# Dropping the allowance for late operands from the planner that orders a decoder block's instructions

## The chip, the cores and the metric

The kernel runs on one NeuronCore of a Trainium2 chip. The metric is the device time of one execution in microseconds (us), median of the runs shown. One profiled execution gives the trace that all rows below come from. PE is TensorE's matmul, PEld its weight load, DVE is VectorE, ACT is ScalarE, POOL is GpSimd, SP is SyncE, whose queue (SPq) issues the transfers. [...]

## The reference

One hybrid decoder layer over 1024 tokens of width 1024, in float32:

```python
xn = rms_norm(x, norm1_g)
q, k, v, p_rw = split(xn @ w_in)
attn = rms_norm(dilated_attention(q, k, v, ...))     # 8 heads of 64, three dilations
rwkv = rwkv7_time_mix(p_rw, ...)                     # 8 heads of 64, a scan over the tokens
x = x + concat(attn, rwkv) @ w_out
xn2 = rms_norm(x, norm2_g)
out = x + (silu(xn2 @ w_gate) * (xn2 @ w_up)) @ w_down
```

The scan keeps a 64x64 state for each head and updates it token by token. The kernel does it in chunks of 64 tokens, so that a chunk is a few matrix products, but one chunk still needs the state that the chunk before it left.

## The kernel before

**Stages.** First come the norm of x and the in-projection (`inproj`, line 524), 26 column blocks by two halves of the tokens; each product of 512 columns is split into three passes of a rounded high and low part. Beside it runs the scan. It has 8 units (four pairs of heads by two halves of the tokens), each prepared by `decays`, `keys`, `scoring`, `sides`, `turn`, `invert` and `merge` (lines 674 to 935) and then walked through by `chain` (line 937), 8 chunks in each unit. Then come attention (`attend`, `near`, `far`, lines 1140 to 1313), the output projection (`outproj`, line 1442) in two rounds, the second norm, and the feed-forward part (`ffproj`, line 1659, then `down`, line 1762), which is the second half of the span.

**The chain.** In each chunk the state goes through three round trips between TensorE and another engine. The product with the state (`chain<-S,ra` in the trace) is copied to Rb by DVE; the product of Rb (`chain<-Rb,M`) is copied to VS by DVE and to Ub by ACT; the products of VS and Ub (`chain<-VS,kbT`, `chain<-Ub,M`) give the new S by DVE, which the next chunk's first product reads. `post` (line 993) turns a unit's result into a part of the mix that the output projection reads.

**The order.** Nothing is scheduled by the compiler; the program itself writes each engine's instructions out in one order, and each engine then takes its own list in that order, with semaphores for the data. The order comes from `Flow`, a list planner that runs while the program is built. Every stage is a generator (a stream) with a rank, a low number being more urgent: norms 2, `feed` 2.5, `chain` 3, the other steps of the scan 3.1 to 3.6, `attn_load` 3.7 and `fetch_wo` 3.8, the workers of attention 8.2 and up, `inproj` 9, `outproj` 9.5. In a loop `Flow.run` (line 237) asks each stream when its next instruction could start (`Flow.ready`, line 180), takes the most urgent of those that could start at the planned time, and otherwise the one that could start first. `Flow.issue` (line 202) books the instruction's planned cost on its engine. So `inproj` fills whatever time TensorE has left.

**When an operand is ready.** For an operand that another engine wrote, `ready` adds to the writer's planned end a lag by engine (line 48) and, if the reader is TensorE, 60 ns and the allowance `LATE`:

```python
LAG = {"PE": 200, "ACT": 145, "DVE": 140, "POOL": 65, "SP": 1500}
LATE, SWITCH = 300, 100
...
r = max(r, t + LAG[e] + (60 + LATE if op.eng == "PE" else 0))
```

A TensorE instruction is thus put into the list where the planner holds its operand to be 300 ns old, beyond the lags. The result is both the place in the order and the planned start, so that what depends on it is planned later too.

**Memory and the joints.** `flow.run(dense)` (line 1346) plans until the in-projection is done. Only then are its pools closed, and the pools of attention are opened in the room that it had: four score buffers, two buffers of queries, three of values. `flow.run(rwkv)` (line 1361) plans on until the scan is done; then the scan's pools are closed, attention gets four more score buffers, and the loads of the output projection (`fetch_wo`, `mix_load`, `residual`) are added. Both kernels have these joints and pools.

Of the kernel before, what the change touches and what calls it, by code (L numbers as in the profile page):

```python
# [47 lines left out]
LAG = {"PE": 200, "ACT": 145, "DVE": 140, "POOL": 65, "SP": 1500}  # L48


LATE, SWITCH = 300, 100
OWN = {"PE": 0, "ACT": 100, "DVE": 130, "POOL": 95, "SP": 900}


# [49 lines left out]
class Flow:  # L104
# [75 lines left out]
    def ready(self, s):  # L180
        op = s.head
        if isinstance(op, Wait):
            if any(m not in self.marks for m in op.marks):
                return None
            return max((self.marks[m] for m in op.marks), default=0.0)
        if isinstance(op, Get):
            t, n = sorted(self.free[op.kind].values()), op.n or 1
            return t[n - 1] if len(t) >= n else None
        r = self.clk.get(op.eng, 0.0)
        if op.eng == "SP":  # L190
            r = max(r, self.clk.get("queues", 0.0) - 3000)
        for keys, which in ((op.rd, 0), (op.wr, 0), (op.wr, 1)):
            for k in keys:
                if k in self.slots:
                    for e, t in self.slots[k][which].items():
                        if e != op.eng or (e == "SP" and (keys is op.rd or which)):
                            r = max(r, t + LAG[e] + (60 + LATE if op.eng == "PE" else 0))
                        elif keys is op.rd and which == 0:
                            r = max(r, t + OWN[e])
        return r  # L200
# [1659 lines left out]
```

## Time and profile before

| What | Value |
|---|---|
| median of 3 runs | 1493.05 us (1490.79 to 1494.58) |
| profiled execution, its own time | 1501.24 us |
| its span, first to last instruction | 1499.4 us |
| PE busy | 1426.3 us, 95% of the span |
| PEld, DVE, ACT, POOL busy | 77%, 53%, 48%, 36% |
| mean granted clock | 0.973 |

A stretch is given as its start and end in us from the first instruction. "Busy" is the time in which an engine executes; the end of a matmul is modelled. A wait row names the engine that waited, the tile that it was to write, and who released it; only idle time of the waiting engine counts in it. Since every instruction is recorded by one helper (line 235, in `Flow.emit`), all rows carry this line, and tiles are what tells the stages apart.

### The profile page before, as it was taken

The page shows a single profiled execution, that of the slowest core. Times are in us where ns is not written, and L with a number is a line of the kernel's source. Part 1 is how long each engine was busy: PE and PEld are TensorE (multiplying, and loading weights), DVE is VectorE, ACT ScalarE, POOL GpSimd, SP SyncE. Part 2 cuts the span into 40 slices and gives each one's busy share as a digit, 9 for nine tenths or more (in the row PEclk, how much of TensorE's full clock was granted, in tenths as well). Part 3 has the DMA queues.
Part 4 walks back from the last instruction along what each step waited for, and adds up shares of the span by engine and source line. Part 5 has one row for each costly group of instructions (what it writes and reads, how often), then busy time and mean ns, then how long its engine had stood idle before and what let it go on. Part 6 is the DMA issues. An engine that isn't in the chain of part 4 may idle for free. (4 is left out here: it accounts for less than half of the span.)

```text
span 1499.4 us, 24765 instructions
## 1 busy us (share of the span) xinstructions
PE 1426.3 (95%) x8710; PEld 1155.9 (77%) x8710; DVE 801.1 (53%) x1799; ACT 714.3 (48%) x1768; POOL 539.8 (36%) x564
## 2 busy tenths in 40 slices
PE   8999989999999986799999899999999999999999
PEld 5677767777778865688888678888888888888887
DVE  5456677657656337666776734443444434334334
ACT  5434556576676775555855433333333333333332
POOL 4432344255645451422454733444444440000000
PEclk8999999999999988799999999999999999999999
DMA  5343222323323344998521222222222224445443
GB/s 192 108 120 75 65 82 78 99 76 110 115 87 103 105 150 125 276 248 224 151 63 50 84 78 85 85 83 79 75 79 80 85 77 134 148 148 197 148 148 126
DMA packets 199789, 173.83 MB, mean 116 GB/s; under 512 B 39025, under 2 KB 150897, under 8 KB 199666
## 3 DMA queue, kind: packets, MB, share of 16 engines
q1 hardware_dynamic: 199666, 172.26, 38.3%
q8 instruction: 69, 1.13, 0.3%
q14 instruction: 54, 0.44, 0.1%
HBM read 130.26 MB, written 37.75 MB: 112 GB/s over the span
## 5 line engine op out<-in xcount | busy, mean ns | idle before, releaser
L235 ACT ACTIVATE oph<-fraw 128x512 fp32r<-128x512 f32 x208 | 126.3, 627 | 228.7 <-PE chain L235 97.9
L235 POOL TENSOR_TENSOR opl<-fraw,oph 128x512 fp32r<-128x512 f32 x76 | 99.6, 1315 | 220.6 <-PE bank L235 71.3
L235 DVE TENSOR_TENSOR opl<-fraw,oph 128x512 fp32r<-128x512 f32 x132 | 87.5, 689 | 143.6 <-ACT oph L235 143.6
L235 ACT ACTIVATE oph<-sw 128x512 fp32r<-128x512 f32 x80 | 50.6, 632 | 179.4 <-DVE sw L235 71.5
L235 POOL TENSOR_TENSOR inlo<-inraw,inhi 128x512 fp32r<-128x512 f32 x62 | 82.2, 1326 | 84.8 <-ACT inhi L235 70.6
L235 PE MATMUL bank<-opl,oph 128*128 128x512 f32 x176 | 68.5, 389 | 0.0
L235 PE MATMUL bank<-oph 128*128 128x512 f32 x176 | 68.5, 389 | 0.0
L235 PE MATMUL bank<-oph,opl 128*128 128x512 f32 x176 | 68.5, 389 | 0.0
L235 DVE TENSOR_TENSOR opl<-sw,oph 128x512 fp32r<-128x512 f32 x80 | 56.0, 699 | 21.0 <-ACT oph L235 17.2
L235 DVE TENSOR_TENSOR uu<-bank,uu 128x512 f32<-128x512 f32 x20 | 13.8, 692 | 81.7 <-PE bank L235 81.7
L235 DVE SCALAR_TENSOR_TENSOR S<-chain,ec,Sp 64x64 f32<-64x64 f32 x112 | 31.6, 282 | 43.1 <-PE chain L235 38.5
L235 ACT ACTIVATE Ub<-chain 64x64 f32<-64x64 f32 x128 | 28.2, 220 | 54.6 <-DVE VS L235 52.4
L235 POOL TENSOR_TENSOR sw<-fraw 128x512 f32<-128x512 f32 x40 | 52.0, 1299 | 0.0
L235 ACT ACTIVATE Y<-chain 64x64 f32<-64x64 f32 x128 | 26.9, 212 | 51.1 <-DVE S L235 45.8
L235 ACT ACTIVATE inhi<-inraw 128x512 fp32r<-128x512 f32 x62 | 38.7, 624 | 16.7 <-DMA inraw<-in_w_in_dram 6.7
L235 DVE COPY Rb<-chain 64x64 f32<-64x64 f32 x128 | 28.9, 226 | 27.9 <-PE chain L235 25.4
L235 POOL TENSOR_TENSOR up<-up,sg 128x512 f32<-128x512 f32 x20 | 32.3, 1617 | 30.1 <-POOL sw L235 16.1
L235 ACT ACTIVATE sb<-sb,mx 128x256 f32<-128x256 f32 (+3 forms) x64 | 36.2, 567 | 14.4 <-DVE mx L235 14.3
L235 PEld LDWEIGHTS bank<-oph,opl 128*128 128x128 f32 x176 | 33.0, 188 | 6.9
L235 PEld LDWEIGHTS bank<-oph 128*128 128x128 f32 x176 | 33.0, 188 | 6.8
L235 PEld LDWEIGHTS bank<-opl,oph 128*128 128x128 f32 x176 | 33.0, 188 | 6.8
L235 POOL TENSOR_TENSOR rsf<-smf,nhalf 128x8 f32<-128x8 f32 x16 | 26.6, 1662 | 31.6 <-DVE smf L235 31.3
(494 smaller groups left out, 4228.6 us busy)
## 6 DMA issues: line engine op xcount, KB each, us to landing
fraw<-in_w_down_dram SPq DMA_DIRECT2D x88, 256.0 KB, 2.8
inraw<-in_w_in_dram SPq DMA_DIRECT2D x62, 256.0 KB, 2.9
fraw<-in_w_gate_dram SPq DMA_DIRECT2D x48, 256.0 KB, 3.7
fraw<-in_w_up_dram SPq DMA_DIRECT2D x48, 256.0 KB, 3.0
fraw<-h_d SPq DMA_DIRECT2D x44, 256.0 KB, 2.9
h_d<-up SPq DMA_DIRECT2D x42, 256.0 KB, 2.1
rkv_d<-stage SPq DMA_DIRECT2D x24, 256.0 KB, 2.9
xt<-in_x_dram SPq DMA_DIRECT2D x8, 512.0 KB, 7.3
```

The source lines that it names most:

```text
L235: op.fn(*op.a, **op.k)
```

## The change

`LATE` is dropped. A TensorE instruction's operand then counts as ready 60 ns plus the writer's lag after the writer's planned end, without the further 300 ns. Nothing else in the program is edited; the same instructions are issued with the same operands, in the order that the planner then writes.

```diff
-LATE, SWITCH = 300, 100
+SWITCH = 100
 OWN = {"PE": 0, "ACT": 100, "DVE": 130, "POOL": 95, "SP": 900}
...
                         if e != op.eng or (e == "SP" and (keys is op.rd or which)):
-                            r = max(r, t + LAG[e] + (60 + LATE if op.eng == "PE" else 0))
+                            r = max(r, t + LAG[e] + (60 if op.eng == "PE" else 0))
                         elif keys is op.rd and which == 0:
```

## Rows read from the trace of the kernel before

**Rows 1.** The page's head: span, and busy time of each engine.
```profile
span 1499.4 us, 24765 instructions
PE 1426.3 (95%) x8710; PEld 1155.9 (77%) x8710; DVE 801.1 (53%) x1799; ACT 714.3 (48%) x1768; POOL 539.8 (36%) x564
```

**Rows 2.** Busy time by stretch: length, engines, granted clock, DMA share, GB/s.
```profile
50.00:550.00 500.00, 479.68 (x4218) 379.05 (x4216) 300.85 (x742) 299.62 (x855) 230.91 (x234) 0.99 0.33 97
550.00:600.00 50.00, 32.11 (x179) 26.60 (x177) 31.43 (x103) 27.59 (x98) 10.10 (x10) 0.80 0.46 133
600.00:850.00 250.00, 227.66 (x1311) 192.74 (x1312) 179.77 (x512) 153.71 (x429) 112.75 (x154) 0.92 0.59 160
850.00:1500.00 650.00, 645.40 (x2821) 529.02 (x2819) 262.95 (x399) 205.26 (x338) 165.18 (x124) 1.00 0.34 108
```

**Rows 3.** The same view, 550 to 600 us in steps of 10 us.
```profile
550.00:560.00 10.00, 5.85 (x25) 4.42 (x24) 2.91 (x10) 7.14 (x23) 4.39 (x5) 0.63 0.44 141
560.00:570.00 10.00, 8.47 (x46) 7.58 (x46) 7.08 (x28) 5.28 (x21) 2.39 (x3) 0.69 0.78 232
570.00:580.00 10.00, 6.67 (x50) 5.41 (x48) 8.76 (x27) 7.54 (x25) 1.30 (x2) 1.00 0.70 188
580.00:590.00 10.00, 7.14 (x40) 6.03 (x39) 6.10 (x20) 5.00 (x18) 0.00 (x0) 0.84 0.36 104
590.00:600.00 10.00, 3.98 (x25) 3.17 (x24) 6.58 (x20) 2.62 (x14) 2.01 (x2) 0.84 0.00 1
```

**Rows 4.** Tiles of in-projection, attention and chain: durations, first and last start.
```profile
L235 PE MATMUL mm<-xn11l,inhi x104: 388/393/628, 53.7 to 547.1; 128*128 128x512 f32 x104
L235 PE MATMUL bank<-kk,qv x104: 222/336/735, 563.6 to 748.8; 128*128 128x128 f32 x44, 128*128 128x384 f32 x24, 128*128 128x256 f32 x20, 128*128 128x512 f32 x16
L235 DVE COPY Rb<-chain x128: 183/227/229, 129.9 to 590.8; 64x64 f32<-64x64 f32 x128
```

**Rows 5.** Instructions in order of time, one round trip at 301 us.
```profile
301.57 0.47 DVE L235 COPY Rb<-chain 64x64 f32<-64x64 f32 x2 [0.52 <-PE chain L235]
...
302.04 0.40 PE L235 MATMUL mm<-xn0h,inlo 128*128 128x512 f32 x1
...
302.28 0.49 PE L235 MATMUL bank<-cs,kb 128*128 128x128 f32 x3
...
302.61 0.39 PE L235 MATMUL chain<-Rb,M 128*128 128x128 f32 x2
```

**Rows 6.** The same view, the same round trip at 585 us.
```profile
585.88 0.23 DVE L235 COPY Rb<-chain 64x64 f32<-64x64 f32 x1
...
586.16 0.49 PE L235 MATMUL chain<-Rb,M 128*128 128x128 f32 x2 [1.26 <-DVE Rb L235]
```

**Rows 7.** Waits of PE, 50 to 550 us (10 groups): us, times, longest.
```profile
PE chain L235 <- DVE S L235: 5.0, 7, 1.9
PE chain L235 <- ACT Ub L235: 4.9, 8, 1.1
...
PE chain L235 <- DVE Rb L235: 1.7, 4, 0.6
...
PE bank L235 <- DVE V L235: 0.4, 1, 0.4
```

**Rows 8.** Waits of PE, 550 to 600 us, the three longest.
```profile
PE chain L235 <- DVE Rb L235: 5.2, 5, 1.4
PE chain L235 <- DVE S L235: 2.7, 4, 1.4
PE chain L235 <- ACT Ub L235: 2.1, 4, 0.9
```

**Rows 9.** PE's groups, 550 to 600 us: one of the chain's five.
```profile
L235 PE MATMUL chain<-Rb,M 128*128 128x128 f32 x14 | 3.9, 364 | 5.3 <-DVE Rb L235 5.2
```

**Rows 10.** Waits of PE, 600 to 850 us (16 groups), first and last.
```profile
PE chain L235 <- ACT sb L235: 6.8, 3, 5.4
...
PE bank L235 <- DVE pt L235: 0.4, 1, 0.4
```

**Rows 11.** Waits of PE, 850 to 1500 us: the only group.
```profile
PE mm L235 <- ACT first L235: 0.3, 1, 0.3
```

## The prediction

> **What bounds the kernel now.** I read the page's head first: PE is busy for 1426.3 of 1499.4 us, every other engine for about half of the span or less [rows 1]. So the sum is made on TensorE alone: a change of order removes no work, it can only change the 73 us in which PE idles and the time that it spends at the lower clock. Next I cut the span into stages [rows 2]. From 850 us on PE idles for 4.6 of 650 us at full clock, and one wait of 0.3 us is all that stands there [rows 11]. From 50 to 550 us, with the in-projection and the scan side by side, it idles for 20.3 of 500 us. From 600 to 850 us it idles for 22.3 of 250 us. [...]
>
> [...] The in-projection's last products start at 547.1 us, attention's first scores at 563.6 us, while the chain's copies to Rb run on from 129.9 to 590.8 us [rows 4]. For 43 us after the filler has ended the chain is still under way, and attention has only four score buffers until it ends. The three longest waits of PE there are the chain's own round trips, 10.0 us together [rows 8]. [...] The chain takes 7.3 us for each of its 64 chunks (460.9 us over 63 steps [rows 4]).
>
> Last, a single round trip. At 301 us the copies to Rb end at 302.04 and their reader starts at 302.61 us; in the 0.57 us between, PE does matmuls of the in-projection and of the scan [rows 5]. At 586 us the last copy ends at 586.11 and the reader starts at 586.16 us, after a wait of 1.26 us [rows 6]. So an operand can be read 0.05 us after its copy. Where there is filler, the order puts the reader about 0.5 us later, and 0.3 us of that is the allowance.
>
> **The change, part by part.** No instruction is added or removed, no transfer either. What moves is each PE instruction that reads what another engine wrote: it stands 300 ns earlier in the planned time, so about one matmul of the in-projection that stood before it now stands behind it. The transfers and the work of the other engines are written in the same planned time, so SP's and POOL's lists move with it; a load is issued earlier where the step before it is planned earlier, and it can't be issued before its buffer is free.
>
> *The chain gains.* Three round trips in each of 64 chunks, at 0.3 us each, are 57.6 us at most. Trips that are stalled already gain nothing, so the bounds are 0 and 57.6 us; I take about half, 29 us, since the copy at 301 us had the whole allowance to give and that at 586 us none. The in-projection ends later by what the chain takes from it: the six or seven chunks that now stand behind it hold five groups of matmuls like that of [rows 9], some 19 us at the clock of the hole. 29 and 19 make 48 us against the 43 us that the chain lags behind, so the chain should end about with the in-projection.
>
> *The hole shrinks.* I leave its first 10 us as they are, since attention must still load its first operands there. In the other four stretches PE idles for 1.5, 3.3, 2.9 and 6.0 us, 13.7 us together, and loses to the lower clock its busy time by one less the clock: 8.47 x 0.31, 7.14 x 0.16 and 3.98 x 0.16, 4.4 us [rows 3]. That is -18 us. The bounds: -24 us, if all of the idle time (17.9 us) and of the clock's loss (32.1 x 0.20 = 6.4 us [rows 2]) goes; and +19 us, if attention's start takes as long as the hole does now and no longer has the chain's 19 us of work to do in it [rows 9]. I take -18, because the waits in the hole are the chain's [rows 8] and the transfers rest at its end.
>
> *Operands come late.* From 50 to 550 us PE has 31 waits on operands in 10 groups, 19.7 us; the chain's three groups have 19 of them, 11.6 us [rows 7]. Each operand that was late with the allowance is later by 0.3 us without it: 31 x 0.3 = 9.3 us. The trace does not show how many others were on time only because of the allowance. The bound below is 0, where one wait covers the next, or where the writer, too, is earlier by what its own operand gained; the bound above takes all of the chain's round trips before the in-projection ends, 57 chunks x 3 x 0.3 = 51 us. I take 9, near the row that counts waits: the round trip of [rows 5] had 0.5 us to spare, so an ordinary one survives the loss of 0.3.
>
> [...] The row shows that PE's idle time before the reader of Rb at 586.16 us was ended by that copy, and no matmul went past it [rows 6]. [...]
>
> *Attention.* From 600 to 850 us PE has 21 waits in 16 groups [rows 10], 17 of them on another engine and the rest on transfers. At 0.3 us each the 17 are 5.1 us more; three of them stand at the start of the feed-forward part, where nothing else is ready and the order doesn't matter. I take +4, between 0 and twice the 5.1.
>
> *The feed-forward part* is costed at nothing. Its products come from one generator after another, so PE's order is the same with and without the allowance, and full buffers of split weights hide what moves on ACT, DVE and POOL (PE busy for 645.4 of 650 us [rows 2]). If that cover were gone, 22 slices of gate and up weights with some seven products each, each 0.3 us late, would be 46 us; the one wait of 0.3 us there [rows 11] says that the cover is far from gone.
>
> *The sum:* -18 + 9 + 4 = -5 us. The profiled execution took 1501.2 us, 1.8 us more than its span and 8.2 us more than the median; against it the sum gives 1496 us, and against the median of 1493.05 us it gives 1488 us. A measurement of this kernel can tell 0.3% from no change, that is 4.5 us, so the forecast stands just beyond it.
>
> **The rivals.**
>
> *Late operands win (slower).* The place is PE from 50 to 550 us: the reader stands in PE's list before its operand, and the filler stands behind it. The mechanism decides once the added waits in all pass the 18 us that the hole gives back. If half of the chain's trips lose their whole allowance there, that is 25 us in place of 9, and the sum is -18 + 25 + 4 = +11, 1504 us. For it: 19 waits of the chain although there was an allowance [rows 7], and DVE and ACT are each busy for 60% of this stretch [rows 2], so that their lists run late now and then. Against it: 0.5 us of slack in an ordinary trip [rows 5].
>
> *The two cancel (no change).* The chain comes forward by less than it lags, because the lists of DVE and ACT pace it and not PE's: half of the hole goes, -9, for the same +13 or somewhat less, 1493 to 1497 us. For it: 7.3 us in a chunk are much more than three trips with the matmuls in them need, so much of a chunk is spent in other engines' lists.
>
> *The hole stays and loses its filler (slower).* Attention's start then is bound by its own loads and buffers. The hole costs +19 in place of -18, and with the 13 us of waits that is +32, 1525 us. For it: a DMA share of 0.78 from 560 to 570 us; against it, 0.00 at the end [rows 3].
>
> *The edit does nothing:* the planner would find PE's list so full that an operand is always old enough, and the order comes out the same, 1493 us. The 0.57 us of filler in [rows 5] speak against it.
>
> **How the numbers follow.** The forecast, with a net gain, gets 0.44; late operands win 0.25; the two cancel 0.20; the hole without filler 0.08; nothing happens 0.03. Faster by over 0.3% is 0.44, within 0.3% is 0.23, slower by over 0.3% is 0.33. The likeliest case reaches from -20 us (the hole's bound of -24 with few new waits) to -4.5 us, 1473 to 1488.5 us, with its sum at the modest end. The range goes on through the cancelled sum to +16 us, where the added waits are 30 us, so 1473 to 1509 us; what lies beyond is the worse part of the late operands and the hole without filler.
>
> **What would show it.** Right: the chain's last copy to Rb starts no later than some 10 us after the in-projection's last product; from 550 to 600 us PE is busy for over 40 us at a clock above 0.9, or the hole is gone; the waits from 50 to 550 us come to some 29 us; attention's first scores start later than 563.6 us, by 10 to 25 us, and the feed-forward part takes the same 650 us. Wrong: the waits from 50 to 550 us above 40 us (late operands), the chain ending where it did against the in-projection (its pace lies elsewhere), or a hole as long as before with PE waiting for loads of queries, keys or score buffers.

## The result, and the profile after

The changed kernel takes 1514.3 us (median of 4 runs, 1513.59 to 1515.45), the kernel before 1493.8 us in the same comparison. The ratio is 1.0141, 95% interval 1.0123 to 1.0158: 21 us slower, where 5 us faster was forecast. The range ended at 1509 us, so it did not hold the time either.

One thing must be known of the profiles. The kernel before varies by some 10 us from one execution to the next, and the profile shown ahead of the prediction came from a long one (1501.24 us). A second profile of the same program, from an execution of 1489.05 us, stands as the first experiment, e1; the profile of the changed kernel is of an execution of 1514.73 us. "Before" below means e1 where nothing else is said, and effects on the whole time are taken from the ratios, not from two profiles.

The head of the page after, to be read against [rows 1]:

```profile
span 1512.9 us, 24796 instructions
PE 1426.3 (94%) x8710; PEld 1146.1 (76%) x8710; DVE 814.1 (54%) x1799; ACT 709.9 (47%) x1768; POOL 537.5 (36%) x564
```

The same 8710 matmuls: as the prediction said, no work was added or removed. That PE is busy for the same 1426.3 us as in [rows 1] is chance; in e1, the same program, it is busy for 1417.7 us. Next the tiles of the in-projection, attention and the chain, which answer to [rows 4]:

```profile
L235 PE MATMUL mm<-xn11l,inhi x104: 387/393/503, 55.0 to 572.2; 128*128 128x512 f32 x104
L235 PE MATMUL bank<-kk,qv x122: 221/280/628, 583.8 to 736.3; 128*128 128x128 f32 x70, 128*128 128x384 f32 x18, 128*128 128x512 f32 x18, 128*128 128x256 f32 x16
L235 DVE COPY Rb<-chain x128: 187/227/230, 132.0 to 566.6; 64x64 f32<-64x64 f32 x128
```

Against the profile of [rows 4], the chain's last copy has come forward from 590.8 to 566.6 us, and the in-projection's last products have gone back from 547.1 to 572.2 us. The two end together, which is what the change was forecast to bring about. Attention's first scores start at 583.8 in place of 563.6 us.

The hole, the 50 us from 550 to 600 us in which PE was busy for 32.11 us at a granted clock of 0.80 [rows 2], did not close, though. The granted clock is given as a share of TensorE's full clock; in the traces of before and after it is either 0.50 or 1.00, and a value between them is a mean over a stretch. After, 128x512 matmuls follow one another after 0.43 us at 0.50 (from 772 us on) and after 0.23 us at 1.00. The same view as [rows 3], after:

```profile
570.00:580.00 10.00, 5.03 (x25) 3.67 (x23) 6.42 (x15) 3.71 (x10) 3.88 (x3) 0.80 0.33 113
580.00:590.00 10.00, 4.20 (x14) 3.54 (x15) 2.36 (x13) 2.40 (x8) 0.00 (x0) 0.50 0.84 262
590.00:600.00 10.00, 6.11 (x24) 5.01 (x23) 7.25 (x19) 7.06 (x17) 2.54 (x2) 0.50 1.01 307
```

It has moved behind the in-projection's new end. These are the 50 us that follow that end, before (e1) and after:

```profile
547.00:597.00 50.00, 32.43 (x180) 26.87 (x179) 31.18 (x100) 27.76 (x99) 10.84 (x10) 0.81 0.47 133
```
```profile
574.00:624.00 50.00, 29.78 (x159) 23.96 (x159) 28.28 (x90) 26.31 (x70) 8.61 (x8) 0.76 0.86 258
```

PE is as idle there as before, but the cause is another. It now waits for transfers, 6.5 us for queries and 3.9 us for the mix, with the granted clock at 0.50 and the DMA share at 0.84 and 1.01 from 580 to 600 us. The longest waits of PE from 574 to 821 us, after, in us, times, longest:

```profile
PE mm L235 <- POOL wol L235: 7.1, 3, 3.1
PE bank L235 <- DMA qv<-qh_d: 6.5, 1, 6.5
PE bank L235 <- DMA mixr<-mix_d: 3.9, 1, 3.9
PE bank L235 <- ACT qv L235: 2.8, 1, 2.8
```

The first of these rows is new. The trace from 759 us on shows it, first PE, then POOL:

```profile
763.06 0.49 PE L235 MATMUL mm<-wol,mh 128*128 128x512 f32 x1 [1.82 <-POOL wol L235]
...
767.21 0.80 PE L235 MATMUL mm<-wol,mh 128*128 128x512 f32 x1 [3.13 <-POOL wol L235]
...
771.02 0.79 PE L235 MATMUL mm<-wol,mh 128*128 128x512 f32 x1 [2.17 <-POOL wol L235]
```
```profile
760.46 2.55 POOL L235 TENSOR_TENSOR wol<-woraw,woh 128x512 fp32r<-128x512 f32 x2
...
764.61 2.54 POOL L235 TENSOR_TENSOR wol<-woraw,woh 128x512 fp32r<-128x512 f32 x2
...
768.43 2.53 POOL L235 TENSOR_TENSOR wol<-woraw,woh 128x512 fp32r<-128x512 f32 x2
```

The second round of the output projection waits for the second half of w_out. That half is split into the buffers that hold the first half, so it can be split only when the first round is done. Before, the first round's last product (the 192nd of 384 with w_out) ended at 730 us, and attention filled the time of the splits until 758 us. After, the first round ends at 758 us and attention at 760 us, so nothing is left to fill it.

Last, the stage beside the scan, from 50 us to the in-projection's end: its length, then busy time and count of matmuls. The kernel before (e1), then after:

```profile
50.00:547.00 497.00, 477.33 (x4208) 377.42 (x4206) 300.90 (x741) 298.10 (x848) 228.72 (x234) 0.99 0.34 97
```
```profile
50.00:574.00 524.00, 496.00 (x4295) 387.54 (x4293) 319.45 (x789) 308.57 (x911) 237.46 (x242) 1.00 0.32 94
```

The stage is 27 us longer. PE's idle time grew by 8.3 us (19.7 to 28.0), the other 18.7 us are shown as busy; but the 87 matmuls that the stage has more are mostly small ones of the chain.

The waits that are shown there come to 27.3 us in 36, against 19.7 us in 31 before [rows 7]. Two of the chain's three lead, after:

```profile
PE chain L235 <- DVE Rb L235: 8.0, 12, 1.7
PE chain L235 <- ACT Ub L235: 7.8, 11, 1.8
```

Waits for Rb were 1.7 us in 4, those for S have fallen from 5.0 us in 7 to 0.9 us in 2. One of the waits for Rb, after:

```profile
208.51 0.63 PE L235 MATMUL mm<-xn11h,inlo 128*128 128x512 f32 x2
...
210.59 0.23 DVE L235 COPY Rb<-chain 64x64 f32<-64x64 f32 x1
...
210.87 0.49 PE L235 MATMUL chain<-Rb,M 128*128 128x128 f32 x2 [1.74 <-DVE Rb L235]
...
211.34 0.71 PE L235 MATMUL mm<-xn11h,inlo 128*128 128x512 f32 x2
```

The in-projection's next products, at 211.34 us, stand behind the reader of Rb in PE's list, and PE idles for 1.74 us before them.

The busy share also hides something. A wait that is shorter than the time by which a matmul's modelled end lies behind the next one's start is not shown as idle. One such place, after:

```profile
154.55 0.46 ACT L235 ACTIVATE Ub<-chain 64x64 f32<-64x64 f32 x2 [3.87 <-DVE VS L235]
154.86 0.19 PEld L235 LDWEIGHTS mm<-xn10h,inlo 128*128 128x128 f32 x1
154.86 0.50 PE L235 MATMUL mm<-xn10h,inlo 128*128 128x512 f32 x1
...
155.06 0.33 PEld L235 LDWEIGHTS chain<-VS,kbT 128*128 128x128 f32 x2
155.20 0.38 PE L235 MATMUL chain<-VS,kbT 128*128 128x128 f32 x2
```

Ub ends at 155.01 us. The wait for it stands at the weight load of the next product in PE's list, which starts at 155.06 us; the product starts at 155.20 us, 0.34 us after the start of the matmul ahead of it, which is shown for 0.50 us, and no idle time is shown. In the feed-forward part such matmuls follow one another after 0.23 us: 2821 of them, nearly all of this shape, in 650 us [rows 2].

To count these as well, I took from the trace for each matmul the time from its start to the next one's start, less the first quartile of the same for its shape (and for a next one of the same or another shape) in e1, and added up what is over. "Lost" below is that sum, whatever the cause, the lower clock included; what is not lost is "work". In the stage beside the scan the work is 392 us before and 405 us after, as the chain's rest came into it; lost are 105.4 and 121.4 us.

Not all of these 16 us are waits for operands. 8.3 us are the idle time that the trace shows, and 1.8 us are the part of those same waits that lies under the modelled end of the matmul ahead. 0.8 us are waits without idle time, where an operand's signal came at most 0.06 us before the product or its weight load. 2.0 us are attention's first wait, which the count lays on the in-projection's last product. The other 3 us end at no operand's signal, and what they are stays open. The difference is not one profile's: the five profiles with 300 ns in this stage (the first, and e1, e3, e4 and e10 of the experiments below) lose 102.9 to 105.9 us there, the five without (after, e2, e9, e13, e17) 120.7 to 127.6 us. In the first 50 us the two groups overlap, at 15.2 to 17.9 and 14.9 to 21.3 us. By stage:

| lost us | before (e1) | after | no allowance beside the scan (e2) | none in attention (e3) |
|---|---|---|---|---|
| 0 to 50 us | 16.2 | 19.3 | 19.2 | 15.3 |
| 50 us to the in-projection's end | 105.4 | 121.4 | 124.3 | 103.9 |
| from there to the feed-forward part | 71.1 | 70.9 | 58.7 | 84.4 |
| its first 90 us | 12.0 | 14.9 | 12.5 | 13.8 |
| the rest | 4.8 | 6.3 | 4.8 | 6.3 |

After minus before is 23.3 us of the 25.6 us between the two spans (1487.3 and 1512.9 us); 2.3 us fall between lost and work. The column of e1 is of a short execution: from the in-projection's end to the feed-forward part the first profile lost 80.6 us where e1 lost 71.1 us, so differences of single profiles in that row are uncertain by some 10 us. In the first 75 us of it the profiles agree better: the first, e1, e4 and e10 lose 44.9 to 46.0 us there, the five without allowance beside the scan 29.6 to 34.6 us.

### The profile page after: what moved, and what is told of

Its sections match the earlier page's. It is cut to its first block, busy times and chain, and to the rows that moved or that the text cites. A ratio compares the mean times of both kernels' runs of the same rounds, so it can differ in the third digit from the quotient of the medians.

```text
span 1512.9 us, 24796 instructions
## 1 busy us (share of the span) xinstructions
PE 1426.3 (94%) x8710; PEld 1146.1 (76%) x8710; DVE 814.1 (54%) x1799; ACT 709.9 (47%) x1768; POOL 537.5 (36%) x564
## 5 line engine op out<-in xcount | busy, mean ns | idle before, releaser
L235 POOL TENSOR_TENSOR opl<-fraw,oph 128x512 fp32r<-128x512 f32 x76 | 100.0, 1318 | 221.7 <-PE bank L235 70.9
L235 ACT ACTIVATE sb<-sb,mx 128x256 f32<-128x256 f32 (+3 forms) x64 | 36.2, 567 | 16.1 <-DVE mx L235 16.1
L235 POOL TENSOR_TENSOR up<-up,sg 128x512 f32<-128x512 f32 x20 | 32.3, 1617 | 32.2 <-POOL sw L235 17.9
L235 DVE TENSOR_TENSOR up<-bank,uu 128x512 f32<-128x512 f32 x30 | 20.8, 692 | 35.4 <-PE bank L235 33.4
L235 PE MATMUL bank<-ra,kb 64*64 64x128 f32 x512 | 38.5, 277 | 0.0
```

Of the source, the lines that this page charges most:

```text
L235: op.fn(*op.a, **op.k)
```

## The experiments

In the edits below, `self.late` is the allowance as a field of the planner, so that it can change at a joint of the program. All verdicts are ratios to the kernel before, run beside each kernel.

### e1: the kernel before, once more

No edit.

> The kernel before, for a second profile, since the first one's execution took 8 us more than the median of its runs. Both theories: a ratio of 1.000 and a time of 1490 to 1496 us. If the excess of the first profile lay in the lower clock between 550 and 700 us, this one shows more than 0.83 of the clock there and the same idle time of PE, 73 us in all; if it lay in idle time, the idle time from 550 to 850 us is under the 40 us of the first.

1493.9 us, ratio 1.0005 (0.9989 to 1.0022). Idle time of PE in the whole span is about 70 us here (1487.3 less the page's 1417.7), against 73 us in the first profile. The lost time behind the in-projection is 71.1 against 80.6 us, that beside the scan 105.4 against 105.9 us. So these two executions of one program differ mostly behind the in-projection. The expectation's two explanations both have a part there: from 550 to 700 us the granted clock is 0.89 here and 0.84 in the first profile, and from 550 to 850 us PE idles for 36.2 and 40.2 us.

### e2, e3, e4: the allowance by stage

```diff
     flow.run(dense)
+    flow.late = 300     # e2, from 0;  e3: from 300, set to 0 here
...
     flow.run(attn)
+    flow.late = 300     # e3;  e4: from 300, set to 0 here
```

> No allowance until the in-projection is planned to its end, 300 ns from there on. Theory S (the loss is made beside the scan: operands late from 50 to 550 us, 7 us, and a start of attention that has lost the chain as its filler): nearly the whole loss stays, 1508 to 1515 us. Theory A (the loss is made in the attention stage, where attention now always goes before the output projection's first round, so that the second half of w_out is loaded and split with nothing beside it): about half or less stays, 1499 to 1505 us, and PE's wait for the split of w_out (7.1 us) is gone.

> 300 ns until the in-projection is planned to its end, none through the rest of the scan, attention and the first output round, 300 ns again behind it. Theory S: 1490 to 1497 us, no change. Theory A: 1500 to 1506 us, with the wait for the split of w_out as in the changed kernel.

> No allowance only behind attention and the first output round: second output round, second norm, feed-forward part. Both theories: 1491 to 1498 us, since PE's order is nearly given there. If the start of the feed-forward part makes the loss (PE idles 9.5 us from 840 to 860 us in the changed kernel, 7.0 from 830 to 850 us in the one before), it is 1496 to 1500 us.

e2: 1.0077 (1.0048 to 1.0106), 11 us. e3: 1.0070 (1.0050 to 1.0089), 10 us. e4: 1.0004 (0.9986 to 1.0021). The parts are additive within their intervals: 0.77 + 0.70 + 0.04 make 1.51%, the change made 1.41%. The medians of e2 and e3 lie in theory A's bounds, but neither theory alone is right: about half of the loss comes with the allowance up to the in-projection's end and half with that in attention's stage, and the feed-forward part has none.

The table says how e2 comes to its 11 us. Beside the scan it loses 18.9 us more than before (with a clock of 0.74 from 260 to 280 us, where the profile after has 1.00), in the first 50 us 3.0 us; behind the in-projection it gains 12.4 us. So the forecast gain is there, with the chain's end at 569.5 and the in-projection's at 575.0 us, but it is smaller than the stage before it pays. In e3 the wait for the splits is there without any change beside the scan (the output projection writes to whichever of the shared banks is free, here one named `chain`):

```profile
PE chain L235 <- POOL wol L235: 5.9, 4, 2.2
```

### e5, e6: the output projection ahead of attention

```diff
-flow.add(9.5, outproj())
+flow.add(8.1, outproj())
```

> The changed kernel with the output projection ranked ahead of attention's workers (8.1 in place of 9.5), so that its first round is no longer left to the end. Theory A1 (in the attention stage the loss comes from the first round ending after attention, so that the loads and splits of w_out's second half have nothing beside them): the wait for the split of w_out, 7.1 us, shrinks to under 2 us, the first round ends well before attention, and the time falls by 6 to 10 us, to 1504 to 1508 us. Rival A2 (the loss there is operands that come late, one by one): 1512 to 1517 us, with the waits on ACT and DVE as before.

> The same rank with the allowance of 300 ns. A1: the first round ends before attention here already, so little is left to gain: 1488 to 1495 us. A2: as well, no change.

1.0376 (1.0351 to 1.0401) and 1.0317 (1.0294 to 1.0340). Both are far slower, and both expectations failed. The first round then ends at 672 and 677 us, but attention only at 824 and 815 us, against 760 and 758 us: with the round's work done early, PE idles for 29.5 us from 672 to 824 us in e5. As a test of the wait for the splits the edit is void, as it changes too much. It fits what the two ranks seem to be for: attention first, the output projection as its filler, and filler left over until the end of attention.

### e7, e8: the chain's products and all others

```diff
-(60 if op.eng == "PE" else 0)
+(60 + self.late * (not (self.first and s.rank == 3)) if op.eng == "PE" else 0)   # e7; e8: s.rank != 3
...
     flow.run(dense)
+    flow.first = False
```

> Until the in-projection is planned to its end, only the chain's own products have no allowance; all other steps keep 300 ns, and all steps have it afterwards. Theory S1 (the loss beside the scan comes with the chain: its operands come late, and it ends before the in-projection, so that attention starts without a filler): nearly the whole of the 11 us, 1501 to 1506 us, chain and in-projection ending within 10 us of each other. Rival S2 (it comes from the other steps' operands): 1491 to 1497 us.

> The counterpart: until the in-projection's end, all steps but the chain's products have no allowance. S1: 1490 to 1496 us, the chain ending some 40 us after the in-projection as in the kernel before. S2: 1500 to 1506 us.

e7: 1.0033 (1.0014 to 1.0051), 5 us. e8: 1.0109 (1.0082 to 1.0137), 16 us. Both medians, 1497.34 and 1508.17 us, lie above the bounds of S2, and S1 failed. The loss of time is more the other steps' than the chain's, which I had not thought: my working of late operands was about the chain's three trips. The first and last starts explain it, the in-projection and the chain of e7, then of e8:

```profile
L235 PE MATMUL mm<-xn11l,inhi x104: 387/393/628, 52.7 to 565.3; 128*128 128x512 f32 x104
L235 DVE COPY Rb<-chain x128: 188/227/229, 128.9 to 576.1; 64x64 f32<-64x64 f32 x128
```
```profile
L235 PE MATMUL mm<-xn11l,inhi x104: 387/395/504, 55.6 to 555.6; 128*128 128x512 f32 x104
L235 DVE COPY Rb<-chain x128: 197/227/229, 132.6 to 598.7; 64x64 f32<-64x64 f32 x128
```

Without an allowance the chain comes forward by 12 us (588.5 in e1 to 576.1) and closes most of the distance to the in-projection: it pays 11.7 us beside the scan, but gets 7.8 us back behind it (63.3 lost in place of 71.1). The other steps pay less there (4.5 us, and 3.6 us in the first 50 us), but get nothing back: the chain, with its own allowance, ends 43 us behind the in-projection as ever, 10 us later. The stage behind loses 77.5 us, which lies between e1 and the first profile; so some 6 of e8's 16 us are not placed.

### e9, e10, e13: w_out's second half left out

```diff
-for m in range(16):              # fetch_wo
+for m in range(8):
...
-for n, k in enumerate(worder):   # load_wo
+for n, k in enumerate(worder[0:4]):
...
-    wo[k] = [T(PO, [128, D], F32R, f"wo{l}{k % 4}") for l in "hl"]
+    wo[k - 4] = wo[k] = [T(PO, [128, D], F32R, f"wo{l}{k % 4}") for l in "hl"]
```

The waits that belong to this half go with it. e9 is the changed kernel with this edit, e10 the kernel before, e13 that of e2.

> The changed kernel without the loads and splits of w_out's second half: the second output round multiplies by the first half again, so this part of the output projection is left out; all products are still made. Theory A1 (in the attention stage the loss is the loading and splitting of that half, which stands between two rounds with nothing beside it): 1502 to 1507 us, 8 to 12 us under the changed kernel, and no wait for a split from 750 to 780 us. Rival A2 (late operands of attention's own steps): 1510 to 1514 us, the 2 to 4 us that the POOL and transfer work saves anywhere.

> The same left out with the allowance of 300 ns. A1: that work lies beside attention here, so it saves little, 1486 to 1491 us, and the distance between this kernel and the one without allowance is 10 to 15 us in place of 21. A2: the distance stays 19 to 22 us.

> No allowance until the in-projection's end and 300 ns behind it, as in the run without it beside the scan (1501.4 us), and w_out's second half neither loaded nor split; the second output round multiplies by the first half again, so that part is left out. Against the run that leaves out the same with no allowance anywhere (1502.9 us) only attention's stage differs. Theory A1 (attention's part of the loss is that half's loading and splitting, alone between two rounds): 1495 to 1499 us, so that 4 to 8 us of attention's 13 are left. Theory A2 (attention's own late operands): 1488 to 1492 us, with 11 to 15 us left.

Ratios: 1.0058 (1.0038 to 1.0078), 0.9940 (0.9924 to 0.9956), 1.0025 (1.0007 to 1.0043). Leaving this out saves 12 us in the changed kernel (1.0141 to 1.0058), 9 us in the one before and 8 us in e2 (1.0077 to 1.0025). The medians of e9, e10 and e13 lie in A1's bounds, but the distance of e9 from e10, 0.0118 or 17.6 us, lies in neither theory's. e13 against e9 is the cleanest, since beside the scan both have one order: with the half in place attention's missing allowance costs 0.0064, 9.6 us; with it left out 0.0033, 4.9 us. So by these ratios about half of attention's part goes with the second half of w_out, and half does not. But each of the two differences is known to some 0.003 only, 4 to 5 us, so the share is not shown.

### e11, e12, e14, e15, e16: other allowances

```diff
-LATE, SWITCH = 300, 100
+LATE, SWITCH = 150, 100        # e11; e12: 500; e14: 75; e15: 225
```

e16 has 150 ns until the in-projection is planned to its end and 300 ns behind it.

> The kernel before with 150 ns in place of 300. If operands that come late cost by how much they are late (theory S), the scan's stage loses about half of its 16 to 19 us and gets back what the chain's earlier end gives: 1497 to 1505 us. If the loss is a matter of two orders that happen to differ, it lies anywhere from 1485 to 1515 us.

> The kernel before with 500 ns. Theory S: fewer waits from 50 us to the in-projection's end, which comes some 5 us earlier, but a chain that ends some 10 us later than it does with 300 ns, with a longer hole behind the in-projection: 1488 to 1500 us. If the allowance were still too small for the operands, and the hole did not matter, it would be 1480 to 1488 us and faster than either kernel.

> The kernel before with 75 ns. Theory S (late operands cost by how late they are; the chain's earlier end closes the hole from 150 ns down): between the runs with 150 ns (1489 us) and without (1514 us), 1496 to 1508 us, the in-projection ending at 569 to 577 us and no hole of the chain behind it. If the order alone decides, by chance, it lies outside.

> The kernel before with 225 ns. Theory S: fewer waits beside the scan than with 150 ns, a chain that ends 10 to 35 us behind the in-projection and a hole that is partly open: 1487 to 1494 us. If the order alone decides, by chance, it lies outside.

> 150 ns until the in-projection is planned to its end, 300 ns from there on. Beside the scan the same order as with 150 ns throughout; behind it attention with the full allowance. If attention's own late operands cost (A2), it is 3 to 6 us faster than 150 ns throughout, 1483 to 1487 us; if 150 ns are enough there, 1487 to 1492 us.

Last starts as in [rows 4], lost time as in the table above:

| allowance, ns | in-projection's last | chain's last copy | lost beside the scan | lost from there to the feed-forward part | ratio |
|---|---|---|---|---|---|
| 500 (e12) | 541.1 | 611.9 | 103.9 | 113.9 | 1.0258 (1.0235 to 1.0281) |
| 300 (e1) | 544.9 | 588.5 | 105.4 | 71.1 | 1.0005 (0.9989 to 1.0022) |
| 225 (e15) | 546.6 | 586.5 | 102.8 | 79.3 | 1.0037 (1.0023 to 1.0052) |
| 150 (e11) | 566.6 | 573.3 | 113.9 | 56.7 | 0.9974 (0.9953 to 0.9996) |
| 75 (e14) | 564.3 | 575.6 | 111.9 | 66.3 | 1.0045 (1.0027 to 1.0062) |
| 0 (after) | 572.2 | 566.6 | 121.4 | 70.9 | 1.0141 (1.0123 to 1.0158) |

Two terms with opposite signs can be seen. Beside the scan more is lost as the allowance falls. Behind it, the hole that the chain leaves is large at 500 ns (the chain ends 71 us behind the in-projection) and nearly gone from 150 ns down. But neither is smooth: from 300 to 225 ns neither end moves much, then they jump by 20 and 13 us; 75 ns lose a little less beside the scan than 150 ns. Theory S missed three of the four times: e11 came out below its bounds, e15 above and e12 far above; e14 lies within, but its in-projection ended earlier than expected. So how much the order alone decides is not separated from the two terms. The order reacts in steps, and what decides where they lie was not found. At 75 ns PE waits for the splits of w_out for 7.2 us again, at 225 and 150 ns for under 1 us, but at 500 ns for 4.5 us. The wait goes with two ends rather than with the size of the allowance: at 75 and 500 ns the first round ends within 5 us of the start of attention's last product, at 225 and 150 ns 17 and 23 us ahead of it.

e16 is the fastest of these: 1488.6 us, 0.9966 (0.9951 to 0.9982), 5 us under the kernel before and 26 us under the changed one, and not to be told from e11; 150 ns are thus enough in attention's stage, as far as these runs can tell. Against e1 it gets 15.4 us back behind the in-projection (55.7 lost) and pays 7.9 us beside the scan (113.3).

### e17, e18: the splits on two engines

```diff
-POOL if n > 3 or h else DVE
+POOL if h else DVE
```

e17 is the changed kernel with this, e18 that of e16.

> The changed kernel with half of the splits of w_out's second half on DVE in place of POOL (0.7 in place of 1.3 us each, and beside POOL's). If the chain of POOL's splits is what the second output round waits for, the wait of 7.1 us falls to 2 to 4 us and the time by 3 to 6 us, to 1508 to 1511 us. If the loads set it, the wait and the time stay, 1513 to 1516 us.

> 150 ns until the in-projection's end, 300 ns behind it, and the same splits on two engines. With 150 ns beside the scan the wait for the splits is 2.1 us; if it goes, the time falls by up to 3 us, to 1485 to 1488 us, and if DVE's share of the splits delays attention's steps instead, it is 1488 to 1493 us.

e17: the wait falls from 7.1 to 2.4 us, so it was the chain of splits and not the loads. But the ratio is 1.0123 (1.0094 to 1.0152): 2.7 us may have been gained, or nothing. The time missed the bounds of the first case. From 740 to 820 us PE idles for 5.4 in place of 9.1 us at the same mean clock; the changed kernel, then e17:

```profile
740.00:820.00 80.00, 70.92 (x372) 56.99 (x371) 56.70 (x99) 40.97 (x97) 31.05 (x44) 0.94 0.19 53
```
```profile
740.00:820.00 80.00, 74.58 (x381) 59.56 (x380) 55.95 (x104) 40.50 (x95) 27.71 (x40) 0.94 0.19 53
```

So the lower level of the granted clock, 0.50 for 10.2 us there in both, does not eat the gain. The two spans still differ by 1.7 us only. Beside the scan, where both have one order, e17's profile lost 5.1 us more, with 20.5 us at the lower level there against 3.4 us; in the first 50 us it lost 4.3 us less. Such differences are as large as the gain looked for. e18: 0.9954 (0.9931 to 0.9977), the lowest ratio of all, but within the interval of e16.

## Why the prediction was wrong

**The bound: right.** TensorE's work did not change, and the feed-forward part, costed at nothing, cost nothing by e4. What the changed kernel loses at its start (2.9 us more in 90 us) is not explained; e2, e3 and e4 have 0.5 to 3.2 us of it.

**The chain gains: right in size.** Taken were 29 us forward for the chain and 19 us back for the in-projection, so that they end together; 24 and 25 us were measured against the first profile, 22 and 27 us against e1. (The five groups that made the 19 us hold 17.9 us in the trace.)

**The hole shrinks by 18 us: the size too large, and the hole stays.** The chain's waits left it as forecast. With the allowance kept in attention, the stage loses 12.4 us less (e2), and in the first 75 us behind the in-projection the profiles lose 10 to 16 us less. But in the first 50 us PE idles for 20.2 us after, 17.6 us in e1. I left the hole's first 10 us as they are "since attention must still load its first operands there". That start then takes longer than 10 us. Without the chain, PE has no work for it, and from 570 to 600 us it idles for 14.7 us at a granted clock of 0.80, 0.50 and 0.50 in its three steps of 10 us, while the loads of attention and of the output projection are asked for within 10 us, from 580 to 590 us. The sign named for being wrong, a hole as long as before with PE waiting for loads of queries, came about. So the rival of a hole that loses its filler, given 0.08, was right on the cause; its price of +19 us was not.

**"Operands come late": the step that failed first.** The working took 31 waits at 0.3 us, 9 us, and called the rest safe since one ordinary trip had 0.5 us of slack. The shown waits did come to 27.3 us, near the "some 29" that were named, but by luck: they are not the same waits, each 0.3 us longer. Waits for Rb went from 4 to 12 with up to 1.7 us each, and those for S nearly vanished. And PE lost 16 us more beside the scan, not 9; 2 of these belong to attention's start, and about half of the 16 is no shown idle time, so the count of waits could not bound it. The 3 us more ahead of 50 us lie within the spread of the profiles. The other steps' products, which I did not work out at all, cost more time than the chain's (16 us in e8 against 5 us in e7), as the chain's earlier end gives some of its cost back. Together, -18 and +9 were to give -9 us for the part up to the in-projection's end; e2 measured +11 us (7 to 16).

**"Attention +4": the step that failed second.** It took the same counting for attention. By e3 this part costs 10 us (7 to 13). Some of it is no late operand of attention: without the allowance attention's products count as ready sooner, and since they are more urgent than the output projection, its first round is pushed to the end of attention; the splits of w_out's second half then have nothing beside them, and PE waits 5.9 us (e3) and 7.1 us (after) for them. That the allowance on the urgent work was also what let the filler in fits e3 and the changed kernel. The prediction did not ask what is late next if attention is done earlier. What the wait costs in the end is open: the ratios of e9 and e13 put it at about half of the part, within their noise, and taking 4.7 us of it away in e17 gave 2.7 us, or nothing. Late operands of attention's own steps are a likely cause of the rest, but were not tried apart.

**No matmul past a waiting one: right in the places shown.** The prediction read at 586.16 us that no matmul went past the reader of a late copy [rows 6]. After, at 210.87 us PE idles for 1.74 us, and the in-projection's products behind that reader do not go ahead; at 763.06, 767.21 and 771.02 us it idles for 1.82, 3.13 and 2.17 us, each time for one split. In both traces, before and after, PE's matmuls start in the order in which the program writes them, as far as their tiles tell them apart.

**The sum in measured terms,** lost time after against before (e1), one profile each: +3.1 in the first 50 us, +16.0 beside the scan, -0.2 from there to the feed-forward part (-12.4 for the hole by e2, +12.2 for attention's missing allowance), +4.4 behind it, 23.3 us; the ratio gives 21 us.

## What to carry to other kernels

In this planner's order the allowance for late operands had two effects of opposite sign: it kept PE, whose matmuls start in the order of its list, from standing before late operands (beside the scan PE idles for 19.7 us with it and 28.0 us without), and it slowed the serial chain by up to its size in each trip (22 of at most 57.6 us). Which of them wins is to be asked for each stage; here 150 ns beside the scan and 300 ns behind it are 0.3% faster than 300 ns everywhere and 1.7% faster than none, and 150 ns everywhere do as well. When urgent work gets faster, look at what the filler was doing meanwhile, and what waits for the filler's end: work that was hidden beside it may come out into the open.

## What was not expected of the hardware

Idle time of PE as the trace shows it is a lower bound of its waiting, since a matmul of 128x512 is shown for 0.39 us while the next starts 0.23 us after it (774.13 and 774.36 us, after). After, beside the scan, 7.1 us lay hidden under the matmuls ahead of the 45 gaps that are shown, 27.9 us, and 2.6 us in waits without any idle time. After, the granted clock was 0.50 from 580 to 600 us; in the 10 us before, where it was 0.80, PE was busy for 5.03 us. And one program's time varied from 1489.05 to 1500.17 us over ten runs, so one profile of a kernel may be 8 us off its median, as much as the effects under study.
